# Seven block products instead of eight for three more pairs of k tiles, with low parts finished by adding transfers

## The chip, the cores and the metric

The kernel runs on one NeuronCore of one Trainium2 chip. The metric is the device time of one execution in microseconds. The engines are TensorE (PE; its weight loads are shown apart as PEld), VectorE (DVE), ScalarE (ACT), GpSimd (POOL) and SyncE (SP), which here only issues transfers.

## What is computed

Two decoder layers on x of 256 tokens by 1024 features, all in float32. Layer 0 mixes tokens with a gated MLP, layer 1 with block-sparse attention; each layer then applies a gated feed-forward network with a causal convolution of width 3, and every sub-layer ends in a layer norm of alpha * x + f(x). The change lies in the feed-forward network:

```
def conv_ffn(x, w_up, conv_w, conv_b, w_down):      # FFN_DIM = 2816
    S = x.shape[1]
    h = x @ w_up                                    # 256 x 1024 @ 1024 x 5632
    hp = jnp.pad(h, ((0, 0), (CONV_WIDTH - 1, 0), (0, 0)))
    hc = conv_b
    for j in range(CONV_WIDTH):
        hc = hc + conv_w[j] * hp[:, j:j + S]
    g, val = jnp.split(hc, 2, axis=-1)
    return (jax.nn.gelu(g) * val) @ w_down          # 256 x 2816 @ 2816 x 1024
...
for i in range(DEPTH):
    ...
    x = layer_norm(DN_ALPHA * x + y, ln_mix_g[i], ln_mix_b[i])
    y = conv_ffn(x, f_w_up[i], f_conv_w[i], f_conv_b[i], f_w_down[i])
    x = layer_norm(DN_ALPHA * x + y, ln_ffn_g[i], ln_ffn_b[i])
```

## The kernel before

**High and low parts.** PE multiplies in a rounded float32 format. Each operand is therefore split into a high part (the rounded copy) and a low part (the value less the copy), and a product is three matmuls: high by high, high by low, low by high. `split` (L388) records the two instructions: a copy on ACT (`act`, L361) and a subtraction on DVE (`tt`, L367).

**Weights.** All weight matrices are one stream of chunks of 128 x 2048 values, 1 MB each. `load` (L385) fetches a chunk on SP's queue, most often into one of two raw buffers; `prep` (L479) splits it into the high and low buffers `whi` and `wlo`, of which there are five pairs (`CHUNKS`). When PE has used a chunk, `spent` (L611) records the `prep` of the one five places on. Chunks in the set `WHOLE` are split in one copy and one subtraction of 2048 columns, the others in pieces. A chunk of the down projection (`f_dn0` in layer 0, `f_dn1` in layer 1) holds two k tiles of 128 x 1024, and there are 11 chunks or 22 k tiles.

**Up projection** (`conv_up`, L1062). Weights of two chunks at a time are the stationary operand, the transposed x the moving one. `gate` (L1089) then makes four convolutions (ACT and DVE), a GELU (ACT), the product with the other half (DVE) and a split of the result into `rr`, which holds all 22 k tiles of activations as high and low parts.

**Down projection** (`project_out`, L885). For k tiles 0 to 15, each k tile is multiplied for both token tiles and both column halves of 512; the last six k tiles (`TAIL`) are then done one token tile after the other, so that the first tile's layer norm runs beside the second tile's products.

**Pairs in seven products.** Two k tiles, two token tiles and two column halves are a product of 2 x 2 blocks, eight block products of three matmuls each. For the chunks in `SEVEN` (L54) the kernel uses seven block products instead, over sums and differences of blocks (Strassen-Winograd). The sums of the activations are made on POOL in the up stage (`token_sums`, L562, instructions at L569) in a kept buffer, and split by `token_parts` (L576). The sums of the weights are made on DVE and split by `weight_sums` (L521). `PART7` (L55) says, for each pair, at which k tile these two are recorded and where their parts are put: in the free halves of the pair's own buffers and `qk`, or in the part of `rr` whose k tiles PE has finished. `seven` (L598) records the products, into four extra accumulators beside the output's; after the last pair `into_rest` (L867) adds the extra ones to the residual. Before the change chunks 5 and 6 of layer 0 and chunks 6 and 7 of layer 1 are such pairs. Of a pair's weights, the first k tile has only its first half split directly (512 columns), the second all of it (1024).

**Order.** Every instruction is recorded with its duration as the author estimates it, and the blocks of memory that it reads and writes. `Plan.emit` (L129) gives each one a due time, counted back from the PE instruction that needs it, simulates the engines as lists that always take the ready instruction with the earliest due time, and emits each engine's instructions in the order so found. PE's products keep the order in which they are recorded. At run time each engine works strictly through its own list.

**Memory.** `place` (L276) gives regions of the big tiles `ff`, `qk` and `rr` to buffers; a new buffer waits for all users of those it overlaps. The up stage keeps its convolutions, gates and joined sums in `ff` up to column 4608. `rowring` is one buffer of 2048 columns for the scale and shift rows of a layer norm (loaded by `ln_rows`, L654), in layer 0 also for the raw chunk of the second pair.

Of the kernel before, what the change touches and what calls it, by code (L numbers as in the profile page):

```python
# [18 lines left out]
P = 128  # L19
# [64 lines left out]
class Plan:  # L84
# [3 lines left out]

    LATE = {"pe": 200.0, "act": 140.0, "dve": 130.0, "pool": 200.0, "sp": 910.0}

# [38 lines left out]
    def emit(self):  # L129
# [28 lines left out]
        engines = ("pe", "act", "dve", "pool", "sp")  # L158
        free = dict.fromkeys(engines, 0.0)
# [12 lines left out]
        while len(order) < len(ops):  # L172
            best = None
            for e in engines:
                c = cand[e]
                if e == "pe":
                    c = [x for x in c if x[1].fill or (nb < len(bulk) and x[1] is bulk[nb])]
                if not c:
                    continue
                s0 = min(max(free[e], r) for r, _ in c)  # L180
                now = [x for x in c if max(free[e], x[0]) <= s0 + 1.0]
                if e == "pe":
                    pick = min(now, key=lambda x: (not x[1].fill, x[1].due))
# [16 lines left out]
            if e == "sp":  # L200
                bus = max(bus, s + 1100.0) + o.nbytes / 360.0
                free[e] = max(s + 475.0, bus - 1500.0)
                o.end = bus
            else:
                extra = 0.0
                if o.table and o.table != table:
                    extra, table = 1300.0, o.table
                o.end = free[e] = s + o.ns + extra
            order.append(o)
            for x in succ.get(o, ()):  # L210
                left[x] -= 1
                if not left[x]:
                    cand[x.eng].append((ready(x), x))
# [18 lines left out]
    def lag(self, d, o):  # L232
        if d.eng == o.eng:
            return 0.0 if d.eng == "pe" else 910.0 if d.eng == "sp" else 130.0
        return self.LATE[d.eng] + (150.0 if o.eng == "pe" else 0.0)
# [10 lines left out]
def trunk_kernel(ctx: ExitStack, tc: tile.TileContext, a: dict, out: bass.AP):  # L246
# [163 lines left out]
    chunks = {}  # L410
    RAW7, DIFF7, KEPT = 0, {"f_dn0": (1536, 1536), "f_dn1": (2048, 3072)}, 4608
    gated = {}
# [21 lines left out]
    def pieces_of(i):  # L434
# [20 lines left out]
        if name == "f_dn1" and c in seven[:1]:  # L455
            loads[i].after = loads[where["b_o", 3]]
        cuts = ((0, HALF), (HALF, SUB)) if i in FINE else ((0, SUB),)
# [6 lines left out]
    def name_k(i, s):  # L464
        name, c = stream[i]
        return name, 2 * c + s

    def with_sums(key, hi, lo, raw, at):

        used = [x.held[0] for x in (xth, xtl)]  # L470
# [35 lines left out]
    for n in ("f_up0", "f_up1"):  # L506
        FINE |= set(range(where[n, 0], where[n, 5]))
    SUMMED = set(range(where["f_dn1", (FT - TAIL) // 2], where["f_dn1", FT // 2 - 1] + 1))

    WHOLE = set()  # L510
    for n in range(2):
# [8 lines left out]

    def weight_sums(name, n):  # L521

        c = SEVEN[name][n]
        raw, (h0, l0), (h1, l1) = loads[name, c], sub(name, c, 0), sub(name, c, 1)
        ah, al = gated["parts"]
        (w11, p11), (w12, p12), (w21, p21), (w22, p22) = ((raw.ap[:, o:o + HALF], range(o // 256, o // 256 + 2))
                                                         for o in range(0, CH, HALF))
        d = place("ff", DIFF7[name][n % 2], SUB)
        both_w = raw.ap.rearrange("p (a b n) -> p a b n", a=2, b=2)
        minus(d.ap.rearrange("p (a n) -> p a n", a=2), both_w[:, :, 1], both_w[:, 0],  # L530
              [(raw, [*p11, *p12, *p22])], [(d, [0, 1])])
        minus(w22, w22, d.ap[:, :HALF], [(raw, p22), (d, [0])], [(raw, p22)])
        minus(w21, w21, w22, [(raw, p21), (raw, p22)], [(raw, p21)])
        kind = PART7[name][n][2]
        if kind == "xt":
            x = xt.rearrange("p (a n) -> p a n", a=4)
            quiet = [Buf(x[:, j], [r.held[0] for r in (xth, xtl)]) for j in range(4)]
            gated.setdefault("xt", []).extend(quiet)
            d13, d42 = ([(b, [0, 1], b.ap) for b in quiet[j:j + 2]] for j in (0, 2))
            split(*d13, (d, [0, 1], d.ap))  # L540
            (d1, d3), (d4, d2) = ([[(b, [j], v[:, j * HALF:(j + 1) * HALF]) for b, _, v in q] for j in range(2)] for q in (d13, d42))
        elif kind == "rr":
# [3 lines left out]
            d4, d2 = ([(b, range(4 + 2 * j, 6 + 2 * j), v[:, j * HALF:(j + 1) * HALF]) for b, _, v in d42] for j in range(2))  # L546
        else:
            d1 = [(b, [2, 3], b.ap[:, HALF:]) for b in (h0, l0)]
# [4 lines left out]
            d4, d2 = ([(b, [j], v[:, j * HALF:(j + 1) * HALF]) for b, _, v in d42] for j in range(2))  # L553
        split(*d42, (raw, [*p21, *p22], raw.ap[:, SUB:]))

# [20 lines left out]
    def token_parts(name, n):  # L576
# [3 lines left out]
        k = PART7[name][n][3]  # L580
        if k is None:
            both = [(b, [2, 3], b.ap[:, HALF:]) for b in sub(name, SEVEN[name][n + 1], 0)]
# [302 lines left out]
    def project_out(name, nk, at, xold, li, rows_i):  # L885

        last = li is None

        rows = None if name in ("b_o", "f_dn0") else ln_rows(rows_i)

# [36 lines left out]
        for k, t in sorted(early, key=lambda x: x[1]) if nk == KT else early:  # L927
# [3 lines left out]
            elif k % 2 and t == NT - 1:  # L931
                n = pairs7.index(k // 2)
                extra = extra or more_banks()
                seven(name, n, own, extra)
                if n == len(pairs7) - 1:
                    into_rest(xold, extra)
# [125 lines left out]
    def conv_up(layer, h, l):  # L1062
        ah, al = place("rr", 0, FT * S), place("rr", FT * S, FT * S)
        av, lv = (b.ap.rearrange("p (f s) -> p f s", f=FT) for b in (ah, al))
        cring = [Places("ff", (j * HALF, 6 * S + j * HALF), HALF) for j in range(2)]
        gring, yring = Places("ff", (4 * S, 22 * S)[:2 - layer], HALF), Places("ff", (6 * S, 8 * S), HALF)
        sring, oring = Places("ff", (10 * S, 12 * S), HALF), Places("ff", (14 * S, 16 * S), HALF)
# [21 lines left out]
        def gate(i, *tiles_, psum=True):  # L1089
# [10 lines left out]
            if kept:  # L1100
                nth = pair.index(i // 2)
                g = gated["kept", nth] = place("ff", KEPT + nth * HALF, HALF)
            else:
# [22 lines left out]
        for t in range(NT):  # L1126
# [305 lines left out]
```

## Time and profile before

| | us |
|---|---|
| median of 3 runs | 558.79 (558.33 to 558.97) |
| the profiled execution | 558.65 |
| span of the profile | 556.5 |
| up stage and down projection, layer 0, by the chain | about 84 to 254.6 |
| the same, layer 1 | about 375 to 541.9 |
| after PE's last product | about 14.6 |

The profile is one execution recorded by the hardware profiler; times count from the start of its span. A row of the chain of waits or of the timeline gives start, length, engine, line and what was done (output<-inputs) with its count. A row of the groups gives line, engine, operation, output<-inputs, shapes and count, then the busy time of the group with the mean of one instruction in ns, then idle time before them and what ended it. A row of the windows gives a stretch and each engine's busy time in it. A row of the DMA issues gives the count, the size of one and the median time from issue to landing. Matmuls overlap their neighbours, so the mean of one matmul is longer than the time from one to the next.

### The profile page before, as it was taken

The page shows a single profiled execution, that of the slowest core. Times are in us where ns is not written, and L with a number is a line of the kernel's source. Part 1 is how long each engine was busy: PE and PEld are TensorE (multiplying, and loading weights), DVE is VectorE, ACT ScalarE, POOL GpSimd, SP SyncE. Part 2 cuts the span into 40 slices and gives each one's busy share as a digit, 9 for nine tenths or more (in the row PEclk, how much of TensorE's full clock was granted, in tenths as well). Part 3 has the DMA queues.
Part 4 walks back from the last instruction along what each step waited for, and adds up shares of the span by engine and source line. Part 5 has one row for each costly group of instructions (what it writes and reads, how often), then busy time and mean ns, then how long its engine had stood idle before and what let it go on. Part 6 is the DMA issues. An engine that isn't in the chain of part 4 may idle for free.

```text
span 556.5 us, 8204 instructions
## 1 busy us (share of the span) xinstructions
PE 549.1 (99%) x3030; PEld 472.1 (85%) x3030; DVE 491.4 (88%) x861; ACT 374.4 (67%) x648; POOL 25.1 (5%) x38
## 2 busy tenths in 40 slices
PE   9999999999999999999999999999999999999995
PEld 6889888988898888888888888788888988888884
DVE  5798989999999999988957778798989988999977
ACT  5657477677777676345667868577777687776841
POOL 0021100000003000001000000000000001002001
PEclk9999999999999999999999999999999999999999
DMA  8988525666654352662656354725846645465302
GB/s 315 389 331 338 218 87 191 238 253 227 225 197 185 151 207 104 238 254 78 232 221 197 101 194 163 293 76 188 322 171 227 227 171 209 156 218 193 114 0 77
DMA packets 19568, 110.97 MB, mean 199 GB/s; under 512 B 2294, under 2 KB 5576, under 8 KB 7368
## 3 DMA queue, kind: packets, MB, share of 16 engines
q1 hardware_dynamic: 19240, 110.18, 53.8%
q8 instruction: 24, 0.39, 0.3%
q10 hardware_dynamic: 288, 0.26, 0.1%
q14 instruction: 16, 0.13, 0.1%
HBM read 109.36 MB, written 1.07 MB: 198 GB/s over the span
## 4 chain that ended last, share of the span: by engine, by line
PE 96%; DVE 2%; DMA 1%; issue 0%; DVEq 0%; ACT 0%; ACTq 0%
PE bank L349 60%; PE twos L349 34%; PE twos L355 1%; PE bank L355 1%; DMA ff<-in_head 1%; DVE x L371 1%; DVE ff L371 0%; DVE stat L721 0%; DVE stat L761 0%; DVE whi L392 0%; DVE ff L764 0%; DVE x L367 0%; DVE x L764 0%; DVEq L1428 0%; DVE x L780 0%
## 5 line engine op out<-in xcount | busy, mean ns | idle before, releaser
L367 DVE TENSOR_TENSOR wlo<-raw,whi 128x1024 fp32r<-128x1024 f32 (+2 forms) x152 | 210.5, 1406 | 17.3 <-ACT whi L361 17.1
L361 ACT ACTIVATE whi<-raw 128x1024 fp32r<-128x1024 f32 (+2 forms) x152 | 176.5, 1194 | 39.6 <-DMA raw<-in_f_up 14.5
L349 PE MATMUL bank<-xt,whi 128*128 128x512 f32 x512 | 121.2, 391 | 0.0
L349 PE MATMUL bank<-whi,rr 128*128 128x512 f32 x382 | 120.9, 391 | 0.0
L349 PEld LDWEIGHTS bank<-xt,whi 128*128 128x128 f32 x512 | 94.7, 188 | 18.7
L349 PEld LDWEIGHTS bank<-whi,rr 128*128 128x128 f32 x382 | 71.8, 188 | 15.3 <-issue 0.3
L349 PE MATMUL bank<-wlo,rr 128*128 128x512 f32 x191 | 74.4, 390 | 0.0
L349 PE MATMUL twos<-xt,whi 128*128 128x512 f32 x320 | 74.4, 390 | 0.0
L371 DVE SCALAR_TENSOR_TENSOR ff<-ff,convc 128x255 f32<-128x255 f32 (+1 forms) x160 | 68.9, 485 | 2.2 <-ACT ff L361 1.9
L349 PEld LDWEIGHTS twos<-xt,whi 128*128 128x128 f32 x320 | 59.5, 188 | 11.9
L349 PEld LDWEIGHTS bank<-xt,wlo 128*128 128x128 f32 x512 | 64.2, 192 | 2.0 <-issue 0.3
L349 PE MATMUL bank<-xt,wlo 128*128 128x256 f32 x512 | 65.7, 284 | 0.0
L361 ACT ACTIVATE ff<-ff,convc 128x256 f32<-128x256 f32 x80 | 44.4, 593 | 5.5 <-DVE ff L367 5.2
L361 ACT ACTIVATE ff<-bank 128x256 f32<-128x256 f32 (+2 forms) x62 | 23.9, 397 | 28.6 <-PE bank L349 27.5
L349 PE MATMUL twos<-whi,xt 128*128 128x512 f32 x128 | 42.1, 396 | 0.0
L349 PEld LDWEIGHTS bank<-wlo,rr 128*128 128x128 f32 x191 | 35.9, 188 | 7.0
L349 PEld LDWEIGHTS twos<-xt,wlo 128*128 128x128 f32 x320 | 39.7, 192 | 0.8
L349 PE MATMUL twos<-xt,wlo 128*128 128x256 f32 x320 | 40.0, 283 | 0.0
L361 ACT ACTIVATE ff<-twos 128x512 f32<-128x512 f32 (+1 forms) x36 | 19.0, 555 | 24.9 <-PE twos L349 21.5
L361 ACT ACTIVATE ff<-bank,lncol 128x128 f32<-128x128 f32 x48 | 18.9, 459 | 22.0 <-PE bank L355 22.0
L349 PEld LDWEIGHTS twos<-whi,xt 128*128 128x128 f32 x128 | 24.1, 188 | 4.7
L361 ACT ACTIVATE rr<-ff 128x512 fp32r<-128x512 f32 (+2 forms) x37 | 21.1, 577 | 7.9 <-DVE ff L367 4.2
(154 smaller groups left out, 610.6 us busy)
## 6 DMA issues: line engine op xcount, KB each, us to landing
raw<-in_f_up SPq DMA_DIRECT2D x44, 1024.0 KB, 4.8
raw<-in_f_dn SPq DMA_DIRECT2D x20, 1024.0 KB, 4.8
raw<-in_b_qk SPq DMA_DIRECT2D x8, 1024.0 KB, 4.7
lnrow<-in_lnrow SPq DMA_DIRECT2D x5, 1024.0 KB, 7.7
raw<-in_a_out SPq DMA_DIRECT2D x4, 1024.0 KB, 6.8
raw<-in_b_v SPq DMA_DIRECT2D x4, 1024.0 KB, 5.5
raw<-in_b_o SPq DMA_DIRECT2D x4, 1024.0 KB, 4.8
raw<-in_a_u SPq DMA_DIRECT2D x3, 1024.0 KB, 6.8
```

The source lines that it names most:

```text
L349: nc.tensor.matmul(o, l, x, start=start, stop=stop)
L355: nc.tensor.transpose(o, x, ident.ap)
L361: return plan.op("act", ns, lambda: nc.scalar.activation(o, x, func, **kw), r, w, table=table)
L367: return dve(70 + 1.04 * flat(x), lambda: nc.vector.tensor_tensor(o, x, y, op=op), r, w)
L371: lambda: nc.vector.scalar_tensor_tensor(o, x, s, y, op0=op0, op1=op1), r, w)
```

## The change

Chunks 4, 5, 6, 7 of layer 0 and chunks 5, 6, 7 of layer 1 are done in seven products: four pairs and three. `PART7` is worked out from a kind for each pair. The kinds `rr` and `qk` are as before; `xt` puts a pair's parts in the transposed-x tile, which is free once the up projection has ended; `early` is new. An early pair, the first of each layer, has its chunk loaded when the up projection is at tile 12 and its weight sums made at tile 14; they stand in `ff` from column 4608 and in `qk`, and only one 512-column split is left for the down projection.

An instruction list `gq` is added to the plan for transfers issued on POOL. In `lows`, ACT writes the negated high part into the low buffer, and a transfer from HBM adds the raw weights to it, so that the DVE subtraction is left out. This is done for the second k tile of all seven pairs (1024 columns each) and for chunk 13 of both up projections and chunk 8 of both down projections (2048 columns each).

Other edits: the kept token sums move to the row buffer, so layer 1's last norm rows are loaded after the pairs; raw chunks of every second pair go to `ff` from column 4096; the up stage of layer 0 has one gate buffer instead of two; the last three chunks of `f_dn1` (and chunk 8 of `f_dn0`) are split whole.

```
-SEVEN = {"f_dn0": (5, 6), "f_dn1": (6, 7)}
-PART7 = {"f_dn0": ((3, 5, "qk", None), (7, 9, "rr", 8)), "f_dn1": ((7, 9, "rr", 8), (9, 11, "qk", 10))}
+SEVEN = {"f_dn0": (4, 5, 6, 7), "f_dn1": (5, 6, 7)}
+KINDS = {"f_dn0": ('early', 'xt', 'rr', 'qk'), "f_dn1": ('early', 'rr', 'qk')}
+def part7(pairs, kinds):
+    out = []
+    for n, (c, kind) in enumerate(zip(pairs, kinds)):
+        at = max(2 * c - 8, {"rr": 7, "qk": 2 * pairs[0] + 1}.get(kind, 1))
+        to = {"rr": 8, "qk": 10}.get(kind, None if pairs[n + 1:] else "own")
+        out.append((at, max(at, 2 * pairs[n + 1] - 8 if to is None else 1 if to == "own" else to + 1), kind, to))
+    return out
+PART7 = {name: part7(pairs, KINDS[name]) for name, pairs in SEVEN.items()}
+ADDED = {"f_up0": {13: "act"}, "f_up1": {13: "act"}, "f_dn0": {8: "act"}, "f_dn1": {8: "act"}}
+BESIDE = SEVEN
...
+            if e == "gq":
+                bus = max(bus, s + 1100.0) + o.nbytes / 360.0
+                free[e] = s + 1200.0
+                o.end = max(bus + 1000.0, s + 2000.0 + o.nbytes / 200.0)
...
-    RAW7, DIFF7, KEPT = 0, {"f_dn0": (1536, 1536), "f_dn1": (2048, 3072)}, 4608
+    RAW7, DIFF7, DIFF_EARLY = 4096, {"f_dn0": (1536, 0), "f_dn1": (2048, 3072)}, 4608
...
-        if c in seven[1:2] and name == "f_dn0":
-            raw = rowring.new()
-        elif c in seven[1:2]:
+        if (name, c) in loads:
+            return [(loads[name, c], 0, HALF, 0), (loads[name, c], 0, SUB, SUB)]
+        if c in seven[1::2]:
             raw = place("ff", RAW7, CH)
...
+    def lows(i, lv, hv, at, hs, ls, by):
+        name, c = stream[i]
+        if by == "act":
+            act(lv, hv.bitcast(F32), AF.Copy, hs, ls, scale=-1.0)
+        else:
+            dve(70 + 0.52 * flat(lv), lambda: nc.vector.tensor_scalar_mul(lv, hv.bitcast(F32), -1.0), hs, ls)
+        plan.op("gq", 3600 + 1.8 * flat(lv), lambda: nc.gpsimd.dma_start(
+            lv, a[name][c][:, at:at + flat(lv)], accum_op=ALU.add, max_dma_last_dim=4 * SUB), (), ls, nbytes=flat(lv) * P * 4)
...
-            tt(lv, raw.ap[:, :CH], hv.bitcast(F32), ALU.subtract, x + hs, ls)
+            by = NEGATED.get(i)
+            if by is None:
+                tt(lv, raw.ap[:, :CH], hv.bitcast(F32), ALU.subtract, x + hs, ls)
+            else:
+                lows(i, lv, hv, 0, hs, ls, by)
...
+            if at and i in SIDE:
+                act(hi.ap, raw.ap[:, at:], AF.Copy, [(raw, range(at // 256, CH // 256))], [(hi, parts)])
+                lows(i, lo.ap, hi.ap, at, [(hi, parts)], [(lo, parts)], "act")
+                continue
...
-    def weight_sums(name, n):
+    def weight_sums(name, n, early=False):
...
+        if early:
+            four = place("ff", DIFF_EARLY + SUB, HALF)
+            minus(w12, w22, d.ap[:, :HALF], [(raw, p22), (d, [0])], [(raw, p12)])
+            minus(four.ap, w21, w12, [(raw, p21), (raw, p12)], [four])
+            d3, d4, d2 = ([(b, [0], b.ap) for b in (place("qk", j * HALF, HALF) for j in q)] for q in ((4, 5), (0, 2), (1, 3)))
+            for q, x in ((d4, (four, [0], four.ap)), (d2, (raw, p12, w12)), (d3, (d, [1], d.ap[:, HALF:]))):
+                split(*q, x)
+            gated["early"] = d, d3, d4, d2
+            return
+        if kind == "early":
+            d1 = [(b, [2, 3], b.ap[:, HALF:]) for b in (h0, l0)]
+            split(*d1, (d, [0], d.ap[:, :HALF]))
...
-        gring, yring = Places("ff", (4 * S, 22 * S)[:2 - layer], HALF), Places("ff", (6 * S, 8 * S), HALF)
+        kept_rows = rowring.new()
+        gring, yring = Places("ff", (4 * S,), HALF), Places("ff", (6 * S, 8 * S), HALF)
...
         for n, i in enumerate(range(2, FT, 2)):
+            if i == 12:
+                pieces_of(where[f"f_dn{layer}", SEVEN[f"f_dn{layer}"][0]])
+            if i == 14:
+                weight_sums(f"f_dn{layer}", 0, early=True)
```

More of the change, by code (lines that the diff above doesn't have):

```diff
@@ L84 @@
 class Plan:
-    LATE = {"pe": 200.0, "act": 140.0, "dve": 130.0, "pool": 200.0, "sp": 910.0}
+    LATE = {"pe": 200.0, "act": 140.0, "dve": 130.0, "pool": 200.0, "sp": 910.0, "gq": 910.0}
     def __init__(self):
@@ L157, in emit @@
                 succ.setdefault(d, []).append(o)
-        engines = ("pe", "act", "dve", "pool", "sp")
+        engines = ("pe", "act", "dve", "pool", "sp", "gq")
         free = dict.fromkeys(engines, 0.0)
@@ L455, in pieces_of @@
         if name == "f_dn1" and c in seven[:1]:
-            loads[i].after = loads[where["b_o", 3]]
+            loads[i].after = loads[where["f_up1", 9]]
         cuts = ((0, HALF), (HALF, SUB)) if i in FINE else ((0, SUB),)
@@ L466, in name_k @@
         return name, 2 * c + s
+    def lows(i, lv, hv, at, hs, ls, by):
[6 more added lines that the diff above has]
+            lv, a[name][c][:, at:at + flat(lv)], accum_op=ALU.add, max_dma_last_dim=4 * SUB), (), ls, nbytes=flat(lv) * P * 4)
     def with_sums(key, hi, lo, raw, at):
-        used = [x.held[0] for x in (xth, xtl)]
+        used = [x.held[0] for x in (xth, xtl)] + gated["xt"]
         x = [Buf(xt[:, o:o + S + 2], used) for o in range(2 * len(wide) * WIDE, (2 * len(wide) + 2) * WIDE, WIDE)]
@@ L489, in prep, with sums @@
             act(hv, raw.ap[:, :CH], AF.Copy, x, hs)
-            tt(lv, raw.ap[:, :CH], hv.bitcast(F32), ALU.subtract, x + hs, ls)
+            by = NEGATED.get(i)
[3 more added lines that the diff above has]
+                lows(i, lv, hv, 0, hs, ls, by)
+            if i in SUMMED:
+                def sums():
+                    for s in range(2):
+                        with_sums(name_k(i, s), *chunks[i][s], raw, s * SUB)
+                if gated.get("x_used") or "xt" not in KINDS["f_dn1"]:
+                    sums()
+                else:
+                    gated.setdefault("x_waits", []).append(sums)
             return
@@ L507, in trunk_kernel @@
         FINE |= set(range(where[n, 0], where[n, 5]))
+    SIDE = {where[n, c] for n, cs in BESIDE.items() for c in cs}
     SUMMED = set(range(where["f_dn1", (FT - TAIL) // 2], where["f_dn1", FT // 2 - 1] + 1))
-    WHOLE = set()
+    NEGATED = {where[n, c]: by for n, cs in ADDED.items() for c, by in cs.items()}
+    WHOLE = set(NEGATED) | SUMMED
     for n in range(2):
@@ L519, in minus @@
         return tt(o, x, y, ALU.subtract, r, w)
-    def weight_sums(name, n):
+    def weight_sums(name, n, early=False):
         c = SEVEN[name][n]
-        raw, (h0, l0), (h1, l1) = loads[name, c], sub(name, c, 0), sub(name, c, 1)
-        ah, al = gated["parts"]
+        raw, kind = loads[name, c], PART7[name][n][2]
         (w11, p11), (w12, p12), (w21, p21), (w22, p22) = ((raw.ap[:, o:o + HALF], range(o // 256, o // 256 + 2))
                                                          for o in range(0, CH, HALF))
[L528 to L534, printed above, removed]
+        if kind == "early" and not early:
+            d, d3, d4, d2 = gated["early"]
+        else:
+            d = place("ff", DIFF_EARLY if early else DIFF7[name][n % 2], SUB)
+            both_w = raw.ap.rearrange("p (a b n) -> p a b n", a=2, b=2)
+            minus(d.ap.rearrange("p (a n) -> p a n", a=2), both_w[:, :, 1], both_w[:, 0],
+                  [(raw, [*p11, *p12, *p22])], [(d, [0, 1])])
+        if early:
[7 more added lines that the diff above has]
+            return
+        (h0, l0), (h1, l1) = sub(name, c, 0), sub(name, c, 1)
+        ah, al = gated["parts"]
+        if kind == "early":
+            d1 = [(b, [2, 3], b.ap[:, HALF:]) for b in (h0, l0)]
+            split(*d1, (d, [0], d.ap[:, :HALF]))
+        else:
+            minus(w22, w22, d.ap[:, :HALF], [(raw, p22), (d, [0])], [(raw, p22)])
+            minus(w21, w21, w22, [(raw, p21), (raw, p22)], [(raw, p21)])
@@ L535, in weight_sums @@
         if kind == "xt":
             x = xt.rearrange("p (a n) -> p a n", a=4)
-            quiet = [Buf(x[:, j], [r.held[0] for r in (xth, xtl)]) for j in range(4)]
-            gated.setdefault("xt", []).extend(quiet)
+            quiet = [Buf(x[:, j], [*(r.held[0] for r in (xth, xtl)), *gated.get("xt", ())]) for j in range(4)]
+            gated["xt"] = quiet
             d13, d42 = ([(b, [0, 1], b.ap) for b in quiet[j:j + 2]] for j in (0, 2))
@@ L553, in weight_sums @@
             d4, d2 = ([(b, [j], v[:, j * HALF:(j + 1) * HALF]) for b, _, v in d42] for j in range(2))
-        split(*d42, (raw, [*p21, *p22], raw.ap[:, SUB:]))
+        if kind != "early":
+            split(*d42, (raw, [*p21, *p22], raw.ap[:, SUB:]))
         def of(b, l, parts, o):
@@ L580, in token_parts @@
         k = PART7[name][n][3]
-        if k is None:
+        if k == "own":
+            both = [(b, [2, 3], b.ap[:, HALF:]) for b in sub(name, c, 0)]
+        elif k is None:
             both = [(b, [2, 3], b.ap[:, HALF:]) for b in sub(name, SEVEN[name][n + 1], 0)]
@@ L887, in project_out @@
         last = li is None
-        rows = None if name in ("b_o", "f_dn0") else ln_rows(rows_i)
+        rows = None if name in ("b_o", "f_dn0", "f_dn1") else ln_rows(rows_i)
         free = [bank(True) for _ in range(2 * NT)]
@@ L934, in project_out @@
                 seven(name, n, own, extra)
+                if name == "f_dn1" and PART7[name][n][2] == "xt":
+                    gated["x_used"] = True
+                    for sums in gated.pop("x_waits", ()):
+                        sums()
                 if n == len(pairs7) - 1:
@@ L1101, in gate @@
                 nth = pair.index(i // 2)
-                g = gated["kept", nth] = place("ff", KEPT + nth * HALF, HALF)
+                g = gated["kept", nth] = Buf(kept_rows.ap[:, nth * HALF:(nth + 1) * HALF], kept_rows.prev)
+                g.ops = kept_rows.ops
             else:
```

6 lines of the change are left out of this document (3 added, 3 removed).

## The prediction

> **What bounds the kernel now.** I read the page first: busy times and the clock, then the chain that ended last.
>
> ```profile
> span 556.5 us, 8204 instructions
> ...
> PE 549.1 (99%) x3030; PEld 472.1 (85%) x3030; DVE 491.4 (88%) x861; ACT 374.4 (67%) x648; POOL 25.1 (5%) x38
> ...
> PEclk9999999999999999999999999999999999999999
> ...
> PE 96%; DVE 2%; DMA 1%; issue 0%; DVEq 0%; ACT 0%; ACTq 0%
> ```
>
> PE is busy almost throughout, at full granted clock, and 96% of the chain is matmuls. Since a busy PE need not be one at its peak, I took the chain in order of time around the first down projection next (start, length, what).
>
> ```profile
> 188.96 11.11 PE twos L349 x64
> 200.07 10.91 PE bank L349 x48
> ...
> 227.48 0.68 PE twos L349 x3
> ...
> 235.64 19.04 PE bank L349 x84
> ```
>
> 84 matmuls of 512 columns take 19.04 us: 0.2267 us each. Three, which are one block product, take 0.68 us, also inside the first pair (227.48), and 48 take 10.91. The rate is the same in a pair as in plain steps, so PE waits for nobody here. Then busy time by stage: up stage and first part of the down projection of layer 0, then that part of layer 1.
>
> ```profile
> 84.00:200.07 116.07, 116.07 (x667) 102.58 (x666) 109.26 (x164) 83.72 (x120) 4.73 (x8) 1.00 0.57 212
> 200.07:232.24 32.17, 32.17 (x144) 26.57 (x143) 31.96 (x45) 21.73 (x27) 0.00 (x0) 1.00 0.40 149
> 491.54:528.90 37.36, 37.36 (x166) 30.92 (x166) 36.05 (x45) 29.50 (x50) 3.66 (x4) 1.00 0.43 155
> ```
>
> The columns are length, PE, weight loads, DVE, ACT, POOL, clock, DMA share and GB/s. PE is never idle, but DVE has only 6.8 us free in 116.07 and 0.2 us in 32.17. So PE is the bound and DVE the engine that could replace it. Time is won by fewer matmuls, and kept only if the extra sums come in time.
>
> **PE's own work.** An ordinary pair of k tiles is 2 k tiles x 2 token tiles x 2 column halves x 3 matmuls = 24. A seven-product pair is 7 x 3 = 21. Layer 0 goes from two such pairs to four, layer 1 from two to three: 3 x 3 = 9 matmuls fewer, 9 x 0.2267 = 2.04 us, 1.36 in layer 0 and 0.68 in layer 1. No other matmul changes. After the last matmul nothing is changed, so all of it reaches the end if PE still never waits.
>
> **DVE and ACT.** Mean ns of one, by shape:
>
> ```profile
> L367 DVE TENSOR_TENSOR wlo<-raw,whi 128x2048 fp32r<-128x2048 f32 x46 | 105.1, 2288 | 8.0 <-ACT whi L361 7.9
> L361 ACT ACTIVATE whi<-raw 128x2048 fp32r<-128x2048 f32 x46 | 87.8, 1909 | 9.1 <-DMA raw<-in_f_up 9.1
> L367 DVE TENSOR_TENSOR wlo<-raw,whi 128x1024 fp32r<-128x1024 f32 x64 | 77.9, 1240 | 7.8 <-ACT whi L361 7.6
> L361 ACT ACTIVATE whi<-raw 128x1024 fp32r<-128x1024 f32 x64 | 65.2, 1053 | 24.8 <-DMA raw<-in_f_dn 5.2 <-PE bank L349 5.1 <-DMA raw<-in_b_v 4.3
> L367 DVE TENSOR_TENSOR wlo<-raw,whi 128x512 fp32r<-128x512 f32 x42 | 27.5, 692 | 1.6 <-ACT whi L361 1.6
> ```
>
> A plain chunk costs DVE one subtraction of 2048 columns, 2.29 us. A seven pair costs 6144 columns: 1536 of low parts, 2048 of sums, 2048 of their low parts, 512 of token sums. Now 1024 of these go to a transfer, so 5120 stay. In columns, layer 0 gets 2 x 4096 more for the two new pairs, less 4 x 1024 (the pairs' second tiles) and less 2 x 2048 (chunk 13 of the up projection, chunk 8 of the down projection): zero. Layer 1: 4096 - 3072 - 4096 = -3072, some 3.4 us less. So DVE is not loaded more as a whole; work is moved. The up stage gets the first pair's early sums, 1.24 + 5 x 0.69 = 4.7 us, and loses 2.29: +2.4 us against 6.8 free. Between 200.07 and the start of the fourth pair (200.07 + 8 x 2.72 + 3 x 4.76 = 236.1) DVE loses the low parts of chunks 4, 7 and 8 (3 x 2.29) and of the second tiles of 5 and 6 (2 x 1.24), 9.3 us; it gains three 512 pieces for pair 4 (2.1) and a whole fourth pair (0.69 + 1.24 + 2 x 0.69 + 2 x 1.24 + 0.69 = 6.5), 8.6 us. 31.96 - 9.3 + 8.6 = 31.3 us for a stretch that is now 36 us. It fits.
>
> ACT gets the copies that PE and the transfers need: 24 x 512 more columns in layer 0, 18 x 512 in layer 1, or 11 and 8 us at 1909 ns per 2048. It has 32 us free in the up stage and 10 in 32.17. Hidden.
>
> POOL gets 12 more token-sum instructions (8 in layer 0, 4 in layer 1). Their group as it is now, the last four of them, and DVE just before these and beside them:
>
> ```profile
> L569 POOL TENSOR_TENSOR ff<-ff 128x128 f32<-128x128 f32 x16 | 10.3, 660 | 237.5 <-DVE rr L367 139.1 <-ACT whi L361 97.9
> ```
>
> ```profile
> 511.30 3.90 POOL L569 TENSOR_TENSOR ff<-ff 128x128 f32<-128x128 f32 x4 [39.95 <-DVE rr L367]
> ...
> 511.05 0.69 DVE L367 TENSOR_TENSOR raw<-raw,ff 128x512 f32<-128x512 f32 x1
> 511.65 0.95 DVE L367 TENSOR_TENSOR wlo<-raw,whi 128x512 fp32r<-128x512 f32 x1
> ```
>
> Beside POOL a 512 subtraction takes 0.95 instead of 0.69 us. Four DVE instructions overlap those four, so I take 0.27 us of DVE per POOL instruction: 2.2 us more in layer 0's up stage. Free time there: 6.8 - 2.4 - 2.2 = 2.2 us. Still enough. [...]
>
> **The adding transfers.** Eleven low parts become a negated copy on ACT and a transfer from HBM that adds the weights: seven of 512 KB, four of 1 MB, all issued on POOL. The trace has no adding transfer, so I bound it by plain ones:
>
> ```profile
> raw<-in_f_dn SPq DMA_DIRECT2D x20, 1024.0 KB, 4.8
> ...
> raw<-in_a_v SPq DMA_DIRECT2D x4, 512.0 KB, 10.5
> ...
> lnrow<-in_f_dn SPq DMA_DIRECT2D x1, 1024.0 KB, 5.9
> ```
>
> From half of 4.8 (2.4, 512 KB moved like a weight chunk) to 10.5 us (512 KB in the crowded start). I take 4.8 for 512 KB, since an add moves the target's bytes too, and 9.6 for 1 MB. [...]
>
> Ten of the eleven have room. A chunk's buffer comes free five chunks ahead: chunk 13's low part is read 11.11 + 7.3 + 1.9 = 20.3 us after that, and load-free preparation takes 2 x 1.91 + 9.6 = 13.4. A transfer that waits on POOL for ACT's negation holds up only token sums (wanted tens of us later); the layer norm's POOL instructions come after the projection. On SP the load of the first pair's chunk moves into the up stage, ahead of loads that are wanted some 20 us later, at a DMA share of 0.57. Layer 1's norm rows are now loaded after the last token sums, as layer 0's are already, and there 84 matmuls run without a gap (row 235.64).
>
> The eleventh is tight: layer 0's fourth pair, chunk 7. Its weights go where chunk 5's were, and chunk 5's go where the last gate's inputs were.
>
> ```profile
> 207.15 2.29 DVE L367 TENSOR_TENSOR wlo<-raw,whi 128x2048 fp32r<-128x2048 f32 x1
> 209.36 2.06 DVE L371 SCALAR_TENSOR_TENSOR ff<-ff,convc 128x254 f32<-128x254 f32 x5
> ...
> 213.67 1.22 DVE L367 TENSOR_TENSOR ff<-raw 128x1024 f32<-128x1024 f32 x1
> ...
> 219.41 1.21 DVE L367 TENSOR_TENSOR qk<-raw,qk 128x1024 fp32r<-128x1024 f32 x1
> ```
>
> The last gate ends at 211.4 now; chunk 4's 2.29 us leave the queue ahead of it, so 209.1. Chunk 5's load then lands 5.9 later (215.0), its sums take what a pair's take now, 213.67 to 220.6, so 6.95 (222.0), chunk 7's load 5.9 (227.9), copies and negation 0.62 + 2 x 1.05 (230.6), the add 4.8: 235.4. PE wants that low part at 236.1 + 0.68 + 0.23 = 237.0. **1.6 us of room**, so I cost it at nothing. If the cover goes, every us beyond 1.6 is a us of PE.
>
> **Sum.** 558.65 is the profiled execution (span 556.5 and 2.15 around it); 558.65 - 2.04 = 556.6. The median of the three runs is 0.14 higher: **556.7**.
>
> **Rivals.** (1) *The late add, slower.* Chunk 7's transfer decides from 4.8 + 1.6 = 6.4 us on, and the kernel gets slower than before from 6.4 + 2.04 = 8.4 us. At 10.5 PE stands 4.1 us and the time is 558.7 - 2.04 + 4.1 = 560.8. For it: 10.5 us in the trace, and chunk 8's whole-chunk add is queued right behind. Against: the 10.5 comes from the first loads of the kernel, which are all wanted at once; here the DMA share is 0.40. Chance 0.15. (2) *DVE becomes the bound or the chain slips by 1 to 3 us, no change.* If POOL's instructions cost DVE twice the row's value, layer 0's up stage lacks 2.2 - 2.2 = 0 us, and the gate, which starts the chain above, slips: without the 2.3 us that I let it move forward and with the add at 6 us, PE stands 2.3 - 1.6 + 1.2 = 1.9 us: 558.6. For it: DVE has 0.2 us free after 200.07. Against: DVE's total falls. Chance 0.16. (3) *The change does not do what it says*, some pair still being multiplied in full: 0.68 us of gain gone for each; the edit lists them plainly, so I give it under 0.02 and count it in (2).
>
> **How the numbers follow.** Forecast 0.69, rival 1 0.15, rival 2 0.16. About 0.2% (1.1 us) is what a measurement of this kernel can tell from no change. The forecast's own range is 556.4 to 557.5 (runs differ by 0.3 around the median; up to 0.9 us of waits). To leave out no more than 2 in 10 it must take in rival 2, 558.6, and its slipping by another 0.6: 556.4 to 559.2. Rival 1 stays outside. Faster 0.69, same 0.16, slower 0.15.
>
> **What would show it.** PE x3021 and the span near 554.4; block products still at 0.68 per three; the four pairs of layer 0 taking 4.76 us each without a gap; DVE's busy time lower by some 3 us apart from overlap with POOL. It is wrong if PE's weight loads wait for a transfer into the low parts (wlo) near 237, if matmuls in the up stage wait for DVE, or if an adding transfer takes over 6.4 us from issue to landing near 231.

## The result and the profile after

The changed kernel takes 563.87 us (median of 4 runs, 562.46 to 564.97) where the kernel before takes 558.76 (558.33 to 558.97): a ratio of 1.0091 (95% interval 1.0075 to 1.0106). It is slower by 5 us. (Ratios here are of the means of the runs.) The profiled execution took 562.46 us, the shortest of the four: the others took 1.2 to 2.5 us more, at a mean granted clock of 0.992 to 0.993 where it has 0.996, and since they left no profile, what they lost more stays open.

First the page of the kernel after: span, busy times, clock by slice, and the chain that ended last.

```profile
span 560.7 us, 8253 instructions
...
PE 549.8 (98%) x3021; PEld 471.4 (84%) x3021; DVE 492.6 (88%) x871; ACT 393.5 (70%) x671; POOL 52.6 (9%) x61
...
PEclk9999999999999999989999999999999999999999
...
PE 89%; DVE 5%; DMA 3%; ACT 2%; issue 1%; POOL 0%; DVEq 0%; ACTq 0%
```

PE has the nine matmuls fewer, yet its busy time is 0.7 us longer, one slice shows a lower clock, and transfers, which held 1% of the chain, now hold 3%. The waits of PE (what was waited for: us in total, times, longest) say which transfer, and the chain in order of time shows how it came to be late.

```profile
PE bank L369 <- DMA wlo<-in_f_dn: 3.3, 1, 3.3
...
PE twos L369 <- DVE xt L387: 0.3, 1, 0.3
```

```profile
226.66 1.82 ACT wlo L381
...
228.85 0.99 POOL wlo L495
229.84 10.81 DMA wlo<-in_f_dn
...
240.70 0.73 PE bank L369 x2
241.43 3.50 PE twos L369 x9
244.93 13.76 PE bank L369 x60
```

The transfer is an adding one, issued at 229.84 and landed at 240.65, 10.81 us later. PE was ready 3.34 us before 240.70, at 237.36, in the second block product of layer 0's fourth pair. What follows is a second loss: nine matmuls take 3.50 us where the same nine of a pair took 2.04 in the chain of before,

```profile
228.84 2.04 PE twos L349 x9
```

and two take 0.73 instead of 0.45. That is 1.74 us, and the windows of the changed kernel show why (length, PE, weight loads, DVE, ACT, POOL, clock, DMA share, GB/s):

```profile
236.20:241.00 4.80, 1.46 (x7) 0.92 (x6) 4.51 (x4) 1.51 (x2) 0.00 (x0) 1.00 1.04 299
241.00:255.00 14.00, 14.00 (x56) 11.37 (x55) 8.74 (x11) 4.61 (x5) 0.00 (x0) 0.88 0.50 201
```

In the first stretch PE works for 1.46 us of 4.80 while the DMA engines are full (share 1.04); in the second the granted clock is 0.88, and 14 x 0.12 = 1.7 us. PE counts as busy all the while, which is why its busy time rose.

ACT's timeline, then POOL's, tell which add came first:

```profile
222.36 1.90 ACT L381 ACTIVATE whi<-raw 128x2048 fp32r<-128x2048 f32 x1
...
225.62 1.05 ACT L381 ACTIVATE whi<-ff 128x1024 fp32r<-128x1024 f32 x1
226.57 2.85 ACT L381 ACTIVATE wlo<-whi 128x2048 fp32r<-128x2048 f32 x2
```

```profile
228.85 2.16 POOL L495 DMA_DIRECT2D wlo<-in_f_dn  x2 [3.91 <-ACT wlo L381]
```

Chunk 8's high part (2048 columns) is copied at 222.36, chunk 7's (1024 columns, from `ff`) only at 225.62, since its load could be issued only at 220.37, behind chunk 5's sums, and landed 5.0 us later. So chunk 8 was ready first: the first of the two negations at 226.57 is 2048 columns wide, chunk 7's 1024 follow, and POOL issues in the same order. The 1 MB add stood ahead of the 512 KB one; the two took 8.4 and 10.8 us.

**Where the 4.2 us of span come from.** Layer 0's first 512-column products end at 258.69 instead of 254.68 (235.64 + 19.04): +4.01 = 0.14 (the products start at 200.21 instead of 200.07) - 1.36 (six matmuls fewer) + 3.34 (the wait) + 1.74 (the clock) + 0.15 left. Layer 1's down projection starts at 496.39 instead of 491.54, so 0.84 us went between: 0.3 of it is the wait for DVE's `xt`, the transposed x behind the layer norm, and the rest was not traced. In layer 1 nothing goes wrong; the chain of before and then that of after:

```profile
491.54 32.67 PE bank L349 x144
...
532.36 9.54 PE bank L349 x42
```

```profile
496.39 27.23 PE bank L369 x120
...
536.53 9.53 PE bank L369 x42
```

From start to end that is 50.36 us before and 49.67 after: 0.69 us, the three matmuls that a third pair saves.

### The profile page after: what moved, and what is told of

The parts are those of the page before. It is cut to its first block, busy times and chain, and to the rows that moved or that the text cites. A ratio compares the mean times of both kernels' runs of the same rounds, so it can differ in the third digit from the quotient of the medians.

```text
span 560.7 us, 8253 instructions
## 1 busy us (share of the span) xinstructions
PE 549.8 (98%) x3021; PEld 471.4 (84%) x3021; DVE 492.6 (88%) x871; ACT 393.5 (70%) x671; POOL 52.6 (9%) x61
## 3 DMA queue, kind: packets, MB, share of 16 engines
q1 hardware_dynamic: 19240, 110.18, 53.3%
q0 software_dynamic: 2096, 7.87, 7.6%
## 4 chain that ended last, share of the span: by engine, by line
PE 89%; DVE 5%; DMA 3%; ACT 2%; issue 1%; POOL 0%; DVEq 0%; ACTq 0%
PE bank L369 55%; PE twos L369 32%; DMA wlo<-in_f_dn 2%; PE twos L375 1%; DVE ff L387 1%; PE bank L375 1%; DVE ff L391 1%; DVE wlo L387 1%; DVE x L391 1%; DMA ff<-in_head 1%; DVE xt L387 0%; ACT ff L381 0%; ACT whi L381 0%; ACT wlo L381 0%; POOL stat L794 0%
## 5 line engine op out<-in xcount | busy, mean ns | idle before, releaser
L387 DVE TENSOR_TENSOR wlo<-raw,whi 128x1024 fp32r<-128x1024 f32 (+2 forms) x141 | 192.5, 1386 | 10.7 <-ACT whi L381 9.9
L381 ACT ACTIVATE whi<-raw 128x1024 fp32r<-128x1024 f32 (+2 forms) x149 | 173.9, 1197 | 24.7 <-DMA raw<-in_f_up 11.3
L369 PE MATMUL bank<-whi,rr 128*128 128x512 f32 x342 | 109.4, 391 | 0.0
L369 PE MATMUL twos<-xt,whi 128*128 128x512 f32 x326 | 76.3, 390 | 0.0
L369 PEld LDWEIGHTS bank<-whi,rr 128*128 128x128 f32 x342 | 64.2, 188 | 13.9 <-DVE rr L387 0.4
L369 PEld LDWEIGHTS twos<-xt,whi 128*128 128x128 f32 x326 | 60.6, 188 | 12.1
L369 PE MATMUL bank<-wlo,rr 128*128 128x512 f32 x171 | 66.7, 390 | 3.3 <-DMA wlo<-in_f_dn 3.3
L369 PE MATMUL twos<-xt,wlo 128*128 128x256 f32 (+1 forms) x323 | 41.1, 284 | 0.0
L369 PEld LDWEIGHTS bank<-wlo,rr 128*128 128x128 f32 x171 | 32.1, 188 | 10.1 <-DMA wlo<-in_f_dn 3.8
L634 POOL TENSOR_TENSOR lnrow<-lnrow 128x128 f32<-128x128 f32 x28 | 27.3, 1013 | 112.6 <-issue 52.5
L387 DVE TENSOR_TENSOR ff<-twos,ff 128x512 f32<-128x512 f32 (+2 forms) x34 | 21.9, 654 | 8.9 <-ACT ff L381 6.9
```

Of the source, the lines that this page charges most:

```text
L369: nc.tensor.matmul(o, l, x, start=start, stop=stop)
L381: return plan.op("act", ns, lambda: nc.scalar.activation(o, x, func, **kw), r, w, table=table)
L387: return dve(70 + 1.04 * flat(x), lambda: nc.vector.tensor_tensor(o, x, y, op=op), r, w)
L634: plan.op("pool", 1200, lambda: nc.gpsimd.tensor_tensor(o, x, y, op=op), r, w)
```

## The experiments

Theory: the fourth pair's add was late because chunk 8's negation and 1 MB add stood ahead of it on ACT, POOL and the DMA engines, and the wait also cost clock. Rivals: an adding transfer of 512 KB takes that long anyway; or DVE, fuller by the early sums and slowed by POOL, makes the chain late. Most edits here make the planner put all engines' lists in a new order, so that a run can lose time far from its edit; where only one list changes it is said.

### Chunk 8's add behind chunk 7's

One order on POOL is turned round and nothing else (chunk 8's negation still goes first on ACT):

```diff
-        plan.op("gq", 3600 + 1.8 * flat(lv), lambda: nc.gpsimd.dma_start(
+        o = plan.op("gq", 3600 + 1.8 * flat(lv), lambda: nc.gpsimd.dma_start(
...
+        gated["gq", name, c] = o
+        if (name, c) == ("f_dn0", 8):
+            o.after = gated["gq", "f_dn0", 7]
```

> Chunk 8's transfer is issued behind chunk 7's instead of ahead of it; all else in the same order (its negation on ACT still comes first). Queue theory: chunk 7's transfer takes 6 to 8 us and lands near 236 to 237.5, PE waits under 1 us, chunk 8's lands just before it is wanted near 241: 557.3 to 558.2. Slow-transfer rival: chunk 7's transfer still takes 10 us, PE waits 2.5 us or more, 560 or more.

558.48 us against 558.91; ratio 0.9996 (0.9986 to 1.0005): 5 us of the loss are gone, but not the gain restored. The DMA issues from 225 to 245, a wait of PE and the chain of this run:

```profile
wlo<-in_f_dn POOLq DMA_DIRECT2D x1, 1024.0 KB, 11.1
...
wlo<-in_f_dn POOLq DMA_DIRECT2D x1, 512.0 KB, 5.4
```

```profile
PE bank L369 <- DMA wlo<-in_f_dn: 1.0, 1, 1.0
```

```profile
230.67 11.08 DMA wlo<-in_f_dn
...
241.80 12.31 PE bank L369 x53
```

The same 512 KB take 5.4 us instead of 10.8 once they are first. The wait left, 1.0 us, is for chunk 8's own add, which now comes last and lands at 241.75. 53 matmuls behind that wait take 12.31 us, 0.3 more than at 0.2267 each: little clock is lost. With only the order of the two issues changed, this shows the queue as the cause: an add of 512 KB is not so slow by itself at this place. (At other places it can be, as the last section has it.)

### Chunk 8's low part on DVE

```diff
-ADDED = {"f_up0": {13: "act"}, "f_up1": {13: "act"}, "f_dn0": {8: "act"}, "f_dn1": {8: "act"}}
+ADDED = {"f_up0": {13: "act"}, "f_up1": {13: "act"}, "f_dn0": {}, "f_dn1": {8: "act"}}
...
-    WHOLE = set(NEGATED) | SUMMED
+    WHOLE = set(NEGATED) | SUMMED | {where["f_dn0", 8]}
```

> Chunk 8 of layer 0 gets its low part from a DVE subtraction again; all other transfers stay. Queue theory (chunk 7's transfer of 512 KB was late because chunk 8's of 1 MB stood ahead of it on ACT, on POOL and in the DMA engines): chunk 7's transfer takes at most 7.5 us instead of 10.8 and starts 2 to 3 us sooner, PE waits under 0.5 us in the fourth pair, the clock stays at 1.00, and the time is 557.0 to 557.8. Rival, a slow transfer (10 us or more at this place whatever stands ahead of it): it still takes 10 us, PE waits 0.5 to 1.5 us, 558 to 559. Rival, DVE bound (the sums are as late as the transfer): with 2.3 us more on DVE PE waits 2 us or more on a DVE instruction, over 559.

558.27 us against 558.91; ratio 0.999 (0.9981 to 1.0). Chunk 7's add takes 5.5 us and PE waits for no transfer in the pairs. Part of the missing gain lies in DVE now:

```profile
PE bank L375 <- DVE x L394: 0.7, 1, 0.7
```

```profile
241.00:255.00 14.00, 14.00 (x66) 11.66 (x65) 13.83 (x20) 4.94 (x6) 0.33 (x1) 1.00 0.72 253
```

DVE is busy 13.83 of 14 us ahead of the layer norm, and PE's transposes (L375) wait 0.7 us for the normed x. Of the 2.04 us due the medians lack 1.4, so this is half of it; the rest is not accounted for. So DVE isn't what made the changed kernel slow, but it has no 2.29 us to give at this place.

### Chunk 7's low part on DVE

```diff
-BESIDE = SEVEN
+BESIDE = {"f_dn0": (4, 5, 6), "f_dn1": (5, 6, 7)}
```

> Chunk 7 of layer 0 (the fourth pair) gets the low part of its second tile from a DVE subtraction; chunk 8 keeps its transfer. Queue theory and slow-transfer rival alike: nothing in the fourth pair waits for a transfer, PE waits under 0.5 us there, 557.0 to 557.8. DVE-bound rival: PE now waits for DVE in the fourth pair by 1.2 us or more, 558.5 or more.

562.75 us against 558.91; ratio 1.0068 (1.0048 to 1.0087). A miss: there is no wait in the fourth pair, yet little is won.

```profile
PE bank L375 <- DVE x L394: 1.6, 1, 1.6
PE bank L369 <- DVE rr L387: 1.5, 1, 1.5
```

The layer norm is 1.6 us late, and in layer 1's attention, some 100 us later, PE waits 1.5 us for DVE's `rr`, a wait that neither the kernel before nor the changed one has. The lists were planned anew, so this run shows that the add can be replaced at its place, and not what that costs by itself.

### The waiting product later

The product that uses chunk 7's late low part is made the sixth of its pair instead of the second, 2.7 us later:

```diff
-        for a, b, to, mine in (("11", "11", extra[0], False), ("12", "21", own[0], True), ("s2", "d2", extra[3], False),
+        for a, b, to, mine in (("11", "11", extra[0], False), ("s2", "d2", extra[3], False),
...
-                               ("s4", "22", own[1], True)):
+                               ("12", "21", own[0], True), ("s4", "22", own[1], True)):
```

> Only the order of the seven products is changed: the product with the late low part comes sixth instead of second, 4 x 0.68 = 2.7 us later. All theories on the transfer: its wait falls from 3.5 to about 0.8 us. Clock theory (the drop of the granted clock to 0.88 over the next 14 us, 1.7 us of PE, comes from the length of the wait): no drop after a wait under 1 us, so 562.5 - 2.7 - 1.7 = 558.0 or less. Without that theory: the clock is still below 1.00 after the pair, and the time is 559.5 or more.

563.58 us against 558.91; ratio 1.0076 (1.0042 to 1.011). A miss again, in an instructive way. The profile is of this kernel's longest execution (569.39 us), so only its order and its wait are read:

```profile
233.58 12.91 DMA wlo<-in_f_dn
...
246.53 16.52 PE bank L369 x59
```

The planner works back from due times. With a later due time it put chunk 7's add at 233.58 instead of 229.84, still behind chunk 8's, and it took 12.91 us: PE waited 5.1. Room given to a transfer whose cost the planner doesn't know is spent again. The clock theory of the expectation is not tested by this run, since the wait grew instead of falling.

### Three pairs in layer 0

```diff
-SEVEN = {"f_dn0": (4, 5, 6, 7), "f_dn1": (5, 6, 7)}
+SEVEN = {"f_dn0": (4, 5, 6), "f_dn1": (5, 6, 7)}
...
-KINDS = {"f_dn0": ('early', 'xt', 'rr', 'qk'), "f_dn1": ('early', 'rr', 'qk')}
+KINDS = {"f_dn0": ('early', 'xt', 'rr'), "f_dn1": ('early', 'rr', 'qk')}
```

> Layer 0 gets three pairs (4, 5, 6) and not the fourth; layer 1 keeps its three. PE issues 3 matmuls more than the changed kernel, so the ideal gain over the kernel before is 2 x 0.68 = 1.36 us: 558.91 - 1.36 = 557.5. Theory (the fourth pair's late add is the loss): PE waits for no add in layer 0's pairs, the clock stays at 1.00, and the time is 557.5 to 558.3, the upper end if chunk 8's add still comes late or the layer norm is late by DVE. Rival (the other parts of the change, the token sums on POOL beside DVE and the early sums, cost the time): 561 or more, without a wait for an add.

557.65 us against 558.65; ratio 0.9991 (0.9975 to 1.0007), a mean clock of 0.999 in the profiled execution and two short waits for adds, 0.3 us for chunk 8's (11.9 us) and 0.2 us for chunk 13's in layer 1's up projection (12.0 us). The median stands 0.36 us over the ideal, but two of the ten runs took over 560 us, and the interval includes no change. For all the rest of the change, early sums, transfers and POOL's sums, it leaves at most 1.8 us over the ideal; the loss of 5 came with the fourth pair.

### No adding transfers

```diff
-ADDED = {"f_up0": {13: "act"}, "f_up1": {13: "act"}, "f_dn0": {8: "act"}, "f_dn1": {8: "act"}}
-BESIDE = SEVEN
+ADDED = {"f_up0": {}, "f_up1": {}, "f_dn0": {}, "f_dn1": {}}
+BESIDE = {}
...
-    WHOLE = set(NEGATED) | SUMMED
+    WHOLE = set(NEGATED) | SUMMED | {where["f_dn0", 8], where["f_dn1", 8]}
```

> All pairs of the change, but every low part is made by a DVE subtraction and no adding transfer is left. DVE gets 4 x 1.24 + 2 x 2.29 = 9.5 us more in layer 0 and 3 x 1.24 + 2 x 2.29 = 8.3 us more in layer 1. If DVE is the limit around the first down projection (13.8 of 14 us busy in 241 to 255 with one or two subtractions more), PE waits for DVE in the pairs or at the layer norm, several us in each layer: 562 or more. If the transfers only cost and DVE has room elsewhere: 557.5 or less, and the adding transfers weren't needed.

575.16 us against 558.65; ratio 1.0295 (1.0269 to 1.0321). PE waits for DVE and ACT in both layers, as the first theory says, but by a way that no expectation names. The two longest waits of PE, and the chain of this run ahead of the first of them:

```profile
PE twos L369 <- ACT qk L381: 4.3, 2, 3.7
PE twos L369 <- ACT xt L381: 1.7, 2, 1.0
```

```profile
227.92 11.15 POOL lnrow L634
...
239.13 0.47 POOL lnrow L634
...
240.69 0.63 ACT rr L381
...
242.26 1.05 ACT qk L381
```

One token sum on POOL takes 11.15 us, from 227.92 to 239.06, and the next ones 0.47. DVE runs two-input subtractions without a gap from 225 to 238.73 and then stands still:

```profile
238.06 0.67 DVE L387 TENSOR_TENSOR ff<-ff 128x512 f32<-128x512 f32 x1
241.35 0.69 DVE L387 TENSOR_TENSOR rr<-lnrow,rr 128x512 fp32r<-128x512 f32 x1 [2.62 <-ACT rr L381]
```

POOL's sum ends 0.33 us after DVE's last subtraction; ACT waits for POOL, and DVE then for ACT. In layer 1 one sum is as long again: 12.34 us, one of the four from 526.27 on. In the changed kernel the longest sum takes 2.39 us. So the adding transfers do more than spare DVE 9.5 us: with them POOL's sums get through. These two sums hold up most, not all, of what PE waits here (some 11 us), and the granted clock, 0.76 from 241 to 255, takes more. The lists were planned anew, so what the transfers alone are worth isn't measured; the run shows that without them, as planned, the added pairs lose 16.5 us.

### Chunk 8's add in halves

Three runs. In the first the planner knows the halves as two transfers, with negation and add of chunk 7 ahead of both; in the second the first half is subtracted on DVE; in the third the lists of the run with chunk 8 behind are kept, and only that one issue becomes two.

```diff
-        plan.op("gq", 3600 + 1.8 * flat(lv), lambda: nc.gpsimd.dma_start(
-            lv, a[name][c][:, at:at + flat(lv)], accum_op=ALU.add, max_dma_last_dim=4 * SUB), (), ls, nbytes=flat(lv) * P * 4)
+        for s in ((0, 1) if (name, c) == ("f_dn0", 8) else (None,)):
+            v, to, w = (lv, at, ls) if s is None else (lv[:, s * SUB:(s + 1) * SUB], s * SUB, [ls[s]])
+            o = plan.op("gq", 3600 + 1.8 * flat(v), lambda v=v, to=to: nc.gpsimd.dma_start(
+                v, a[name][c][:, to:to + flat(v)], accum_op=ALU.add, max_dma_last_dim=4 * SUB), (), w, nbytes=flat(v) * P * 4)
...
+                o.after = gated["gq", "f_dn0", 7]
```

> Chunk 7's add ahead of chunk 8's, and chunk 8's 1 MB add in two of 512 KB, the half that PE uses first issued first. If what was left with the whole chunk behind was the 1.0 us wait for chunk 8's add (11.1 us for 1 MB), the first half lands some 4 to 5 us sooner, PE doesn't wait, and the time is 558.5 - 1.0 = 557.5 (557.0 to 557.8). If the rest of the missing gain is DVE's (layer norm, transposed x late) the wait goes and the time stays: 558.2 to 558.6.

```diff
+                tt(lv[:, :SUB], x.ap[:, :SUB], hv[:, :SUB].bitcast(F32), ALU.subtract, [(x, range(4)), hs[0]], [ls[0]])
+                act(lv[:, SUB:], hv[:, SUB:].bitcast(F32), AF.Copy, [hs[1]], [ls[1]], scale=-1.0)
...
+        for s in ((1,) if (name, c) == ("f_dn0", 8) else (None,)):
```

> Chunk 7's add ahead of chunk 8's; the first half of chunk 8's low part (k tile 16) by a DVE subtraction of 1.24 us, only the second half by an add of 512 KB. No wait for an add is expected. If DVE has 1.2 us of room between 222 and 241: 557.0 to 557.6. If DVE is full there, its queue is late by up to 1.2 us at the layer norm, and the time is 558.2 to 558.8, as with the whole subtraction.

```diff
-        o = plan.op("gq", 3600 + 1.8 * flat(lv), lambda: nc.gpsimd.dma_start(
-            lv, a[name][c][:, at:at + flat(lv)], accum_op=ALU.add, max_dma_last_dim=4 * SUB), (), ls, nbytes=flat(lv) * P * 4)
+        step = SUB if (name, c) == ("f_dn0", 8) else flat(lv)
+        o = plan.op("gq", 3600 + 1.8 * flat(lv), lambda: [nc.gpsimd.dma_start(
+            lv[:, o:o + step], a[name][c][:, at + o:at + o + step], accum_op=ALU.add, max_dma_last_dim=4 * SUB)
+            for o in range(0, flat(lv), step)], (), ls, nbytes=flat(lv) * P * 4)
```

> As the run with chunk 7's add ahead of chunk 8's, in which every engine keeps its order, but chunk 8's add goes out as two adds of 512 KB, issued back to back. Against the run with halves that was planned anew (560.8, with a 1.5 us wait for DVE's rr in layer 1's attention, where the lists of all engines had changed), this one has the lists of the 558.5 run. If the wait in attention comes from the new lists and the 1.0 us wait came from the 1 MB add: neither wait is left, and the time is 557.3 to 557.8. If the attention wait comes from the pairs being done sooner: it's there again, 559 or more. If two halves land no sooner than one whole: 558.5.

The three took 560.82 (ratio 1.0039, 1.0024 to 1.0054), 560.76 (1.0038, 1.0026 to 1.005) and 559.75 us (1.002, 1.0005 to 1.0034). In the first two no wait for an add is left and all four pairs run through. Waits of PE in the first:

```profile
PE bank L369 <- DVE rr L387: 1.5, 1, 1.5
```

That is the wait in attention again. The third keeps the old lists and does not have it; it has this instead, and the second line gives its three adds from issue to landing (shortest, median, longest, which is also their order of issue):

```profile
PE bank L369 <- DMA wlo<-in_f_dn: 1.8, 1, 1.8
```

```profile
DMA to landing us min/median/max: 5.4/8.2/12.1
```

Chunk 7's 512 KB land after 5.4 us, the first half after 8.2, the second after 12.1: the same queue in smaller pieces lands its last byte no sooner than one whole (11.1). (In the first run, with other lists, the halves took 6.7 and 9.6 us.) PE wants the second k tile 0.68 us after the first, so halves give it little. Of the three outcomes expected, "no sooner" is what happened, but not with the 558.5 us that go with it: the time is 1.3 us above the run with the whole chunk; part of that is the longer wait, part clock, 0.88 from 241 to 255 in the profiled execution. That the attention wait belongs to certain new lists is likely, since the run with the old lists lacks it, but PE also came there at another time, and other newly planned kernels (chunk 8 on DVE, three pairs) lack it too, so it isn't shown.

### Three pairs with halves

The same edit of the issue in the kernel with three pairs.

> Three pairs in layer 0, with the lists of the 557.65 run, and chunk 8's add as two adds of 512 KB. Its ideal is 1.36 us under the kernel before; it waited 0.3 us for chunk 8's add. Without that wait: 557.3. If the four pairs with halves come out lower than this by 0.3 to 0.7, the fourth pair is worth its 0.68 us; if not, three pairs are the better change.

557.05 us against 558.64; ratio 0.9977 (0.9966 to 0.9988). The page's span and chain:

```profile
span 554.7 us, 8236 instructions
...
PE 97%; DVE 2%; issue 0%; DVEq 0%; ACT 0%; ACTq 0%
```

This beats the kernel before by 1.3 us (0.7 to 1.9), which is the 1.36 of six matmuls, and no wait of PE for an add, DVE or ACT is left. Against three pairs with the whole add (0.9991, 0.9975 to 1.0007) the intervals overlap. No version with four pairs came below 558.2.

### Another chunk by transfer

Chunk 8 stays on DVE; chunk 2, or chunk 3, of the same down projection, both wanted before the pairs, gets the 1 MB add:

```diff
-ADDED = {"f_up0": {13: "act"}, "f_up1": {13: "act"}, "f_dn0": {}, "f_dn1": {8: "act"}}
+ADDED = {"f_up0": {13: "act"}, "f_up1": {13: "act"}, "f_dn0": {2: "act"}, "f_dn1": {8: "act"}}
```

> Four pairs, chunk 8's low part by DVE as in the 558.27 run, but chunk 2 of the same down projection, whose buffers come free some 20 us before PE wants it, gets its low part by a 1 MB add. DVE is spared 2.29 us at about 195 and chunk 7's add has the queue to itself. If the late layer norm of the 558.27 run was DVE's queue alone: PE waits neither for an add nor at the layer norm, and the time is 558.65 - 2.04 = 556.6 to 557.2. If DVE's relief at 195 is lost again before 241 (it then waits for ACT or for loads): 558.0 to 558.4. If chunk 2's add lands late: a wait near 211, 559 or more.

> As the run with chunk 2 added, but with chunk 3, whose buffers come free at about 200 and which PE wants at about 216.6: DVE is spared its 2.29 us nearer to where it is full (21.5 of 21.8 us from 200 to 222). If the add lands in 11 us there's 1 to 3 us of room: 556.6 to 557.2. If it meets chunk 5's and 6's adds in the queue: PE waits near 217, 559 or more.

570.47 (ratio 1.0209, 1.0193 to 1.0225) and 561.57 us (1.0046, 1.003 to 1.0063) against 558.73. Neither helps. With chunk 2 the add itself isn't waited for, but a small load beside it is. The chain of this run, then that of the run with three pairs at the same load:

```profile
205.18 7.19 DMA ff<-in_onehot
...
214.05 0.33 PE twos L772
214.39 12.52 PE bank L369 x48
```

```profile
202.08 1.65 DMA ff<-in_onehot
```

The load for the attention's bias table (`in_onehot`, 49.5 KB) takes 7.19 instead of 1.65 us with the DMA share at 0.97 from 200 to 222; PE waits 3.5 us, and the 48 matmuls behind it take 12.52 us instead of 10.91. That is 5.1 of some 12 us. Of the rest, 1.5 is the wait in attention and 3.7 are waits for DVE and ACT in layer 1's down projection, where the clock is 0.94 from 495 to 546; why these come was not traced. With chunk 3 the add of chunk 7 is late again by 1.2 us (PE goes on at 238.83), and the layer norm by 0.9.

## Why the prediction was wrong, step by step

- **PE's own work: right.** Nine matmuls fewer, 0.68 us per block product, 0.69 us saved in layer 1, and 1.3 us measured in the kernel with three pairs and halves where 1.36 were due.
- **The chain up to the fourth pair: right.** Negation to end at 230.6, PE to want the part at 237.0; the add was issued at 229.84 and PE stood from 237.36. The load landed 2.5 us sooner than the text has it (225.4), and chunk 8's negation on ACT took 1.82 us of that.
- **The step that failed: "the add 4.8: 235.4", with "1.6 us of room, so I cost it at nothing".** It took 10.81. At this place, alone or first, it takes 5.4 to 5.5 us (five later runs show it), which would have landed at 235.2 to 236.1; the size of one add was near enough. The 4.8, twice the 2.4 of a load, was the author's estimate; the runs show the doubling in the time on the DMA engines, 0.97% of the span for a MB of adds and 0.48% for a MB of loads. What was wrong is the place in the queue. The text has "chunk 8's whole-chunk add is queued right behind"; it was queued right ahead, and so was its negation on ACT. The likely reason was at hand: the planner takes what is ready, and the same chain has chunk 7's load as late as 227.9, while chunk 8's waits for nothing of the kind.
- **"Ten of the eleven have room": wrong for chunk 8's.** With chunk 7's add in front, PE waits 1.0 us for chunk 8's. Two adds of 1.5 MB together have to land between 230 and 241, with loads for layer 1's attention in between. The DMA share is 0.99 there (229.80 to 240.70), where the text argued with 0.40, that of the stretch before the change. With the 1 MB in one piece either order left one of them late.
- **Rival 1 named the place and the condition**, an add over 6.4 us, and nearly its size (10.5), though not the order that caused it. At 560.8 us it was priced without what a wait does to the clock: 3.34 + 1.74 us instead of 4.1, and 0.84 lost between the down projections.
- **"DVE and ACT", "it fits": right in what it cost**, since PE waits 0.3 us for DVE, but with less room than the text has. From 200.07 to 236.10 DVE is busy for 35.61 us, not 31.3, and 12 of layer 0's 16 token sums run there and not ahead of 200.07. DVE's busy time did not fall by 3 us apart from overlap with POOL. It is 492.6 against 491.4, and the token sums run beside it:

```profile
L634 POOL TENSOR_TENSOR lnrow<-lnrow 128x128 f32<-128x128 f32 x28 | 27.3, 1013 | 112.6 <-issue 52.5
```

Their mean is 1013 ns where it was 660. How much DVE time goes there was not tried. What rival 2 feared shows as soon as DVE gets one low part back: a layer norm 0.7 to 1.6 us late.

## What to carry to other kernels

Before a transfer is costed at nothing, write down what its queue does ahead of it, on every engine of its chain, by the order that is really emitted: here an add of 512 KB took 10.8 us behind one of 1 MB and 5.4 ahead of it. And price a wait of PE with its clock: here 1.8 and 3.3 us of waiting cost 1.9 and 1.7 us more, while 1.0 and 1.6 us cost 0.3. The last pair of such a change can eat the gain of the others: try the change with one part fewer.

## What the runs showed of the hardware that was not expected

In the changed kernel the adding transfers kept the DMA engines busy twice as long for each MB as the loads. The page of the changed kernel gives packets, MB and share of 16 engines' span for SP's queue and for POOL's:

```profile
q1 hardware_dynamic: 19240, 110.18, 53.3%
q0 software_dynamic: 2096, 7.87, 7.6%
```

53.3 / 110.18 = 0.48% a MB for loads, 7.6 / 7.87 = 0.97% for adds. How long one add takes seems to go with how full the DMA engines are. Of the seven of 512 KB in the changed kernel, those issued at 202.53, 217.16 and 520.10 took 5.6, 5.5 and 6.0 us at a DMA share of 0.90, 0.70 and 0.68 from issue to landing; those at 512.08, 504.83, 221.20 and 229.84 took 7.3, 9.5, 8.2 and 10.8 us at 0.92, 0.93, 1.01 and 0.99. The row of the one at 504.83:

```profile
wlo<-in_f_dn POOLq DMA_DIRECT2D x1, 512.0 KB, 9.5
```

So the 5.4 us of chunk 7's add in front of chunk 8's is no constant of the transfer. 1 MB took from 8.0 us (layer 0) to 13.4 (layer 1) in one run alone, that with chunk 7's low part on DVE. Three adds issued back to back, chunk 7's and chunk 8's halves in the old lists, landed in turn (5.4, 8.2, 12.1 us).

One of POOL's token sums in the run without transfers took 11.15 us, all but the last 0.33 of it beside DVE's two-input subtractions without a gap (layer 0), and one took 12.34 (layer 1); the sums that followed the first of them, with DVE standing, took 0.46 to 0.47. Why POOL's sum took so long there, and not where DVE worked beside it in the changed kernel (2.39 us at most), isn't shown.

The clock after a wait of PE: after 0.98 us (chunk 8's add behind) 0.3 us are lost; after 1.55 us (attention, halves) also 0.3, twelve matmuls taking 3.02 instead of 2.72; after 1.81 us (halves in the old lists) fifty take 13.27 instead of 11.33; after 3.34 us 1.74 are lost, with matmuls up to 0.43 us apart instead of 0.2267. So 1.81 us of waiting cost as much clock as 3.34; what sets the loss isn't shown.
